# Top-2 gate and dispatch on one core: 15 transfers instead of 24, equal groups of 64 rows, and a share of the multiplication on ScalarE

## The chip, the core and the metric

The kernel runs on one core of one Trainium2 chip. The metric is the device time of one execution in microseconds, as the median of several runs. A profile of one execution (a trace) stands beside it; its span reaches from the first to the last instruction.

## The reference

For each of 16,384 tokens a softmax over 8 router logits is taken, the two largest probabilities are kept and divided by their sum, and the token's row of 512 floats is written twice, each copy multiplied by one of the two weights (the smaller weight first):

```python
# x: [16, 1024, 512] f32, router_logits: [16, 1024, 8] f32, k = 2
probs = softmax(router_logits)
topk_indices = np.argsort(probs, axis=-1)[..., -k:]
topk_probs = np.take_along_axis(probs, topk_indices, axis=-1)
topk_probs = topk_probs / np.sum(topk_probs, axis=-1, keepdims=True)
x_expanded = x[:, :, np.newaxis, :].repeat(k, axis=2)
return (x_expanded * topk_probs[..., np.newaxis]).astype(np.float32)
```

So 33.6 MB of x and 0.5 MB of logits are read and 67.1 MB are written.

## The kernel before

Each of the 128 partitions holds 128 tokens ("rows" below: one row is one token on each partition, 256 KB to load and 512 KB to store over all partitions). The rows come in two groups, GROUPS = [65, 63]; in a group, each partition's rows lie side by side in device memory, so that one transfer has one contiguous piece per partition.

**Buffers.** `xs` holds the x rows of one group, and is used again for the second one. `osp` holds L = 16 output rows. Output rows that have no place in `osp` are written over x rows of `xs` that are no longer needed: `over(r, n, G)` gives the place: two x rows for each output row, from x row 2r - G on.

**Loads.** The x rows of the first group come in six transfers of 2, 4, 2, 8, 17 and 32 rows, those of the second in three of 16, 16 and 31 (LOADS, line 112). After the first two (6 rows) come the logits of all 128 rows, in two transfers (lines 116 and 117). All are issued on SyncE's queue (SP), which works through its instructions in the program's order.

**Weights.** `top2_weights` reduces the 8 logits to the largest and second largest in a tournament of VectorE (DVE) max and min instructions (lines 27 to 40). The two normalised weights are sigmoids of plus and minus their difference, by ScalarE (ACT, lines 42 and 43). This happens once, for all 128 rows.

**Multiplications and stores.** In each group DVE multiplies in pieces, one instruction each (line 128), and each piece is stored by one transfer (line 136): 2 and 14 rows into `osp`, 16 rows over `xs`, two times 8 rows into `osp` again, and the rest over `xs` (9 and 8 rows in the first group, 15 in the second, LAST). The 2-row piece is the early store: it goes out on ACT's queue, all others on SP's. The second use of `osp` waits until its first contents have been stored, and the loads of the second group wait until the output over those rows of `xs` has been stored. Nothing else orders the engines; the framework puts in these waits from the regions that instructions read and write.

Of the kernel before, what the change touches and what calls it, by code (L numbers as in the profile page):

```python
# [1 line left out]

# [4 lines left out]

F32 = mybir.dt.float32
ALU = mybir.AluOpType
ACTF = mybir.ActivationFunctionType  # L10
P = 128


def top2_weights(nc, pool, logits, M, E, tag=""):

    hi, lo, n = None, None, E  # L20
    while n > 1:
        n //= 2
        if hi is None:
            a, b = logits[:, :, 0:n], logits[:, :, n : 2 * n]
            nhi = pool.tile([P, M, n], F32, tag=f"hi{n}{tag}")
            nlo = b
            nc.vector.tensor_tensor(nhi, a, b, op=ALU.max)  # L27
            nc.vector.tensor_tensor(nlo, a, b, op=ALU.min)  # L28
        else:
            a, b = hi[:, :, 0:n], hi[:, :, n : 2 * n]  # L30
            nhi = pool.tile([P, M, n], F32, tag=f"hi{n}{tag}")
            nlo = pool.tile([P, M, n], F32, tag=f"lo{n}{tag}")
            tmp = pool.tile([P, M, n], F32, tag=f"tmp{n}{tag}")
            nc.vector.tensor_tensor(tmp, lo[:, :, 0:n], lo[:, :, n : 2 * n], op=ALU.max)  # L34
            nc.vector.tensor_tensor(nlo, a, b, op=ALU.min)  # L35
            nc.vector.tensor_tensor(nlo, nlo, tmp, op=ALU.max)  # L36
            nc.vector.tensor_tensor(nhi, a, b, op=ALU.max)  # L37
        hi, lo = nhi, nlo
    dlt = pool.tile([P, M], F32, tag=f"dlt{tag}")
    nc.vector.tensor_tensor(dlt, hi[:, :, 0], lo[:, :, 0], op=ALU.subtract)  # L40
    WA = pool.tile([P, M, 2], F32, tag=f"WA{tag}")
    nc.scalar.activation(WA[:, :, 0], dlt, ACTF.Sigmoid, scale=-1.0)  # L42
    nc.scalar.activation(WA[:, :, 1], dlt, ACTF.Sigmoid, scale=1.0)  # L43
    return WA

GROUPS = [65, 63]

LOADS = [[2, 4, 2, 8, 17, 32], [16, 16, 31]]


LAST = [[(48, 9), (57, 8)], [(48, 15)]]


@with_exitstack
def kernel(
    ctx: ExitStack,
    tc: tile.TileContext,  # L60
    x: bass.AP,
    router_logits: bass.AP,
    k: bass.AP,
    out: bass.AP,
):
    nc = tc.nc
    B, S, D = x.shape
    E = router_logits.shape[-1]
    N = B * S
    assert int(k) == 2 and E == 8 and N == P * sum(GROUPS)  # L70
    M = N // P

    L = 16
    x_v, o_v, rl_v = [], [], []
    t0 = 0
    for n in GROUPS:
        t1 = t0 + P * n
        x_v.append(
            x.rearrange("b s d -> (b s) d")[t0:t1].rearrange("(p m) d -> p m d", p=P)
        )  # L80
        o_v.append(
            out.rearrange("b s k d -> (b s) k d")[t0:t1].rearrange(
                "(p m) k d -> p m k d", p=P
            )
        )
        rl_v.append(
            router_logits.rearrange("b s e -> (b s) e")[t0:t1].rearrange(
                "(p m) e -> p m e", p=P
            )
        )  # L90
        t0 = t1

    wpool = ctx.enter_context(tc.tile_pool(name="wpool", bufs=1))
    logits = wpool.tile([P, M, E], F32)
    xs = wpool.tile([P, max(GROUPS), D], F32)
    osp = wpool.tile([P, L, 2, D], F32)

    def over(r, n, G):

        a = 2 * r - G
        return xs[:, a : a + 2 * n, :].rearrange("p (r k) d -> p r k d", k=2)

    h = L // 2
    e = 2
    m0 = 0
    for g, G in enumerate(GROUPS):
        r = 0  # L110
        for n in LOADS[g]:
            nc.sync.dma_start(xs[:, r : r + n, :], x_v[g][:, r : r + n, :])  # L112
            r += n
            if g == 0 and r == 6:

                nc.sync.dma_start(logits[:, :G], rl_v[0])  # L116
                nc.sync.dma_start(logits[:, G:], rl_v[1])
                WA = top2_weights(nc, wpool, logits, M, E)
        assert r == G
        begin = [(0, e, osp[:, :e]), (e, L - e, osp[:, e:])]  # L120
        plan = begin + [
            (L, L, over(L, L, 2 * L)),
            (2 * L, h, osp[:, :h]),
            (2 * L + h, h, osp[:, h:]),
        ]
        plan += [(r, n, over(r, n, G)) for r, n in LAST[g]]
        for r, n, og in plan:
            nc.vector.tensor_tensor(  # L128
                og,
                xs[:, r : r + n, :].unsqueeze(2).to_broadcast([P, n, 2, D]),  # L130
                WA[:, m0 + r : m0 + r + n, :].unsqueeze(3).to_broadcast([P, n, 2, D]),
                op=ALU.mult,
            )

            queue = nc.scalar if n == e else nc.sync
            queue.dma_start(o_v[g][:, r : r + n], og)
        m0 += G


# [1 line left out]
_INS = ['x', 'router_logits', 'k']  # L141
_OUTS = [((16, 1024, 2, 512), 'float32')]

_NUMBERS = {'k': 2}


# [26 lines left out]
```

## Time and profile before

| what | value |
|---|---|
| time, 3 runs | median 240.15 us (239.95 to 240.82) |
| span of the profiled execution | 239.1 us |
| time that lies around the span, by the median | 1.0 us |
| DVE busy | 142.1 us, 24 instructions |
| ACT busy | 1.8 us, 3 instructions |
| moved by DMA | 101.19 MB, mean 423 GB/s over the span |
| SP's queue | 96.5% of the span's DMA time, 3168 packets |
| ACT's queue | 2.1%, 288 packets |

The profiled execution's time is not listed apart from the three runs; its span with 1.0 us around it is taken for the median. The DMA time of a queue is the time that its packets took, as a share of what the 16 DMA engines of the core have in the span. A packet here is one contiguous piece of one partition, or the small write that tells a transfer's end. For a transfer "to landing" is the time from its issue until all 16 engines have reported its end.

### The profile page before, as it was taken

How to read it: one execution, taken by the hardware profiler on the slowest of the kernel's cores; microseconds unless marked ns; L12 is line 12 of the kernel's file. 1: busy time of each engine (PE TensorE's matmuls, PEld its weight loads, DVE VectorE, ACT ScalarE, POOL GpSimd, SP SyncE). 2: the span in 40 equal slices, each digit the busy share in tenths (PEclk: the TensorE clock that was granted, in tenths of full speed). 3: DMA queues.
4: the chain of work that ended last, by engine and by line, in shares of the span. 5: the costliest groups of instructions: out<-in, count | busy, mean ns of one | idle time of the engine just before them, and what ended most of it. 6: DMA issues, size and time to landing. Idle time of an engine off the chain costs nothing.

```text
span 239.1 us, 118 instructions
## 1 busy us (share of the span) xinstructions
DVE 142.1 (59%) x24; ACT 1.8 (1%) x3; POOL 0.2 (0%) x4
## 2 busy tenths in 40 slices
DVE  0589999900299699900000699999006999990000
ACT  2000000000000000000000000000000000000000
POOL 0000000000000000000000000000000000000000
DMA  7999989899999999999999999899899898999894
GB/s 254 440 463 426 441 388 526 329 460 460 417 438 406 400 422 438 438 481 396 433 438 438 438 511 396 384 502 394 384 460 515 362 493 367 428 433 486 380 483 175
DMA packets 3456, 101.19 MB, mean 423 GB/s; under 512 B 384, under 2 KB 512, under 8 KB 896
## 3 DMA queue, kind: packets, MB, share of 16 engines
q1 hardware_dynamic: 3168, 99.09, 96.5%
q10 hardware_dynamic: 288, 2.10, 2.1%
HBM read 34.08 MB, written 67.11 MB: 423 GB/s over the span
## 4 chain that ended last, share of the span: by engine, by line
DMA 52%; DVE 33%; issue 4%; SPq 1%; ACT 0%; DVEq 0%
DMA out_dram<-xs 24%; DVE xs L128 18%; DVE osp L128 13%; DMA out_dram<-osp 13%; DMA xs<-in_x_dram 13%; DMA logits<-in_router_logits_dram 3%; SPq L112 0%; DVE nhi L27 0%; DVE logits L28 0%; DVE nlo L36 0%; DVE nhi L37 0%; DVE nlo L35 0%; DVE tmp L34 0%; SPq L116 0%; ACT WA L42 0%
## 5 line engine op out<-in xcount | busy, mean ns | idle before, releaser
L128 DVE TENSOR_TENSOR osp<-xs,WA 128x8192 f32<-128x8192 f32 (+2 forms) x8 | 69.2, 8688 | 62.3 <-DMA xs<-in_x_dram 31.2
L128 DVE TENSOR_TENSOR xs<-xs,WA 128x16384 f32<-128x16384 f32 (+3 forms) x5 | 69.1, 13811 | 2.2 <-DMA out_dram<-xs 2.0
L27 DVE TENSOR_TENSOR nhi<-logits 128x512 f32<-128x512 f32 x1 | 0.7, 691 | 8.5 <-DMA logits<-in_router_logits_dram 8.5
L42 ACT ACT_TABLE_LOAD x1 | 1.3, 1283 | 0.7 <-PEq L154 0.7
L28 DVE TENSOR_TENSOR logits<-logits 128x512 f32<-128x512 f32 x1 | 0.7, 691 | 0.0
L35 DVE TENSOR_TENSOR nlo<-nhi 128x256 f32<-128x256 f32 (+1 forms) x2 | 0.7, 351 | 0.0
L37 DVE TENSOR_TENSOR nhi<-nhi 128x256 f32<-128x256 f32 (+1 forms) x2 | 0.7, 351 | 0.0
L36 DVE TENSOR_TENSOR nlo<-nlo,tmp 128x256 f32<-128x256 f32 (+1 forms) x2 | 0.7, 350 | 0.0
L34 DVE TENSOR_TENSOR tmp<-logits 128x256 f32<-128x256 f32 x1 | 0.4, 417 | 0.0
L42 ACT ACTIVATE WA<-dlt 128x128 f32<-128x128 f32 x1 | 0.3, 315 | 10.4 <-DVE dlt L40 10.4
L40 DVE TENSOR_TENSOR dlt<-nhi,nlo 128x128 f32<-128x128 f32 x1 | 0.3, 291 | 0.0
L43 ACT ACTIVATE WA<-dlt 128x128 f32<-128x128 f32 x1 | 0.3, 298 | 0.0
L34 DVE TENSOR_TENSOR tmp<-nlo 128x128 f32<-128x128 f32 x1 | 0.3, 283 | 0.0
L154 POOL MEMSET const-bfloat16-1.0<- 128x1 bf16 x1 | 0.1, 101 | 0.0
L154 POOL MEMSET const-uint8-127<- 128x1 uint8 x1 | 0.1, 101 | 0.0
L154 POOL MEMSET const-float32-0.0<- 128x1 f32 x1 | 0.1, 98 | 0.2 <-issue 0.2
L154 POOL MEMSET const-float32-1.0<- 128x1 f32 x1 | 0.1, 98 | 0.0
## 6 DMA issues: line engine op xcount, KB each, us to landing
out_dram<-osp SPq DMA_DIRECT2D x4, 4096.0 KB, 20.7
out_dram<-osp SPq DMA_DIRECT2D x2, 7168.0 KB, 32.4
xs<-in_x_dram SPq DMA_DIRECT2D x2, 4096.0 KB, 30.4
xs<-in_x_dram SPq DMA_DIRECT2D x1, 7936.0 KB, 40.9
out_dram<-xs SPq DMA_DIRECT2D x1, 7680.0 KB, 23.1
out_dram<-xs SPq DMA_DIRECT2D x1, 4608.0 KB, 20.4
xs<-in_x_dram SPq DMA_DIRECT2D x1, 4352.0 KB, 22.8
out_dram<-xs SPq DMA_DIRECT2D x1, 4096.0 KB, 21.4
```

What stands on the lines that cost most here:

```text
L27: nc.vector.tensor_tensor(nhi, a, b, op=ALU.max)
L28: nc.vector.tensor_tensor(nlo, a, b, op=ALU.min)
L34: nc.vector.tensor_tensor(tmp, lo[:, :, 0:n], lo[:, :, n : 2 * n], op=ALU.max)
L35: nc.vector.tensor_tensor(nlo, a, b, op=ALU.min)
L36: nc.vector.tensor_tensor(nlo, nlo, tmp, op=ALU.max)
L37: nc.vector.tensor_tensor(nhi, a, b, op=ALU.max)
L40: nc.vector.tensor_tensor(dlt, hi[:, :, 0], lo[:, :, 0], op=ALU.subtract)
L42: nc.scalar.activation(WA[:, :, 0], dlt, ACTF.Sigmoid, scale=-1.0)
L43: nc.scalar.activation(WA[:, :, 1], dlt, ACTF.Sigmoid, scale=1.0)
L128: nc.vector.tensor_tensor(og, xs[:, r : r + n, :].unsqueeze(2).to_broadcast([P, n, 2, D]), WA[:, m0 + r : m0 + r + n, :].unsqueeze(3).to_b ...
L154: nc = _bacc.Bacc("TRN2", target_bir_lowering=False, num_devices=1)
```

## The change

- GROUPS becomes [64, 64].
- The loads of both groups become 16, 16 and 32 rows. The logits come after the first 16 rows, in one transfer.
- The stores of each group become four of 16 rows: into `osp`, over `xs`, into `osp`, over `xs`. There is no 2-row store on ACT's queue any more; all transfers are on SP's.
- In the third store of each group DVE multiplies 12 rows and ACT the other 4, with eight instructions (each row has two copies) of 512 elements per partition, whose scale is the row's weight.
- The logits and the scratch of the tournament are no tiles of their own: they lie in rows 15 to 17 of `osp`, which has 18 rows now. The weights keep a tile.

The transfers: 3 + 1 + 4 in the first group and 3 + 4 in the second, 15 together, where the kernel before has 8 + 7 and 3 + 6.

```diff
-GROUPS = [65, 63]
-LOADS = [[2, 4, 2, 8, 17, 32], [16, 16, 31]]
-LAST = [[(48, 9), (57, 8)], [(48, 15)]]
+GROUPS = [64, 64]
+M = sum(GROUPS)
+LOADS = [[16, 16, 32], [16, 16, 32]]
+STORES = [
+    [(16, 0, 0), (16, None, 0), (16, 0, 4), (16, None, 0)],
+    [(16, 0, 0), (16, None, 0), (16, 0, 4), (16, None, 0)],
+]
+EARLY = 2
+OSP = 18
...
+    logits = osp[:, OSP - 1].rearrange("p k d -> p (k d)").rearrange("p (m e) -> p m e", e=E)
+    scratch = osp[:, OSP - 3 : OSP - 1].rearrange("p r k d -> p (r k d)")
+    def load_logits():
+        nc.sync.dma_start(
+            logits.rearrange("p (g m) e -> p g (m e)", g=2),
+            rf.rearrange("(g p m) e -> p g (m e)", g=2, p=P),
+        )
...
         for n in LOADS[g]:
             nc.sync.dma_start(xs[:, r : r + n, :], x_v[g][:, r : r + n, :])
+            if g == 0 and r == 0:
+                load_logits()
+                top2_weights(nc, scratch, logits, WA)
             r += n
-            if g == 0 and r == 6:
-                nc.sync.dma_start(logits[:, :G], rl_v[0])
-                nc.sync.dma_start(logits[:, G:], rl_v[1])
-                WA = top2_weights(nc, wpool, logits, M, E)
...
+        for n, home, by_act in STORES[g]:
+            if home is None:
+                a = 2 * r - (r + n)
+                og = xs[:, a : a + 2 * n, :].rearrange("p (r k) d -> p r k d", k=2)
+            else:
+                og = osp[:, home : home + n]
+            v = n - by_act
+            w = WA[:, m0 + r : m0 + r + n, :]
             nc.vector.tensor_tensor(
-                og,
+                og[:, :v],
...
                 op=ALU.mult,
             )
+            for i in range(v, n):
+                for c in range(2):
+                    nc.scalar.activation(
+                        og[:, i, c], xs[:, r + i, :], ACTF.Copy, scale=w[:, i, c : c + 1]
+                    )
+            queue = nc.scalar if n == EARLY else nc.sync
             queue.dma_start(o_v[g][:, r : r + n], og)
+            r += n
```

The tournament in `top2_weights` keeps its instructions and their shapes; only the places of its intermediate results change.

More of the change, by code (lines that the diff above doesn't have):

```diff
@@ L11, with top2_weights, cut @@
 P = 128
-def top2_weights(nc, pool, logits, M, E, tag=""):
-    hi, lo, n = None, None, E
+E = 8
+D = 512
+GROUPS = [64, 64]
[7 more added lines that the diff above has]
+OSP = 18
+def top2_weights(nc, scratch, logits, WA):
+    used = [0]
+    def cut(n):
+        a = scratch[:, used[0] : used[0] + M * n].rearrange("p (m n) -> p m n", n=n)
+        used[0] += M * n
+        return a
+    a, b = logits[:, :, 0:4], logits[:, :, 4:8]
+    hi = cut(4)
+    lo = b
+    nc.vector.tensor_tensor(hi, a, b, op=ALU.max)
+    nc.vector.tensor_tensor(lo, a, b, op=ALU.min)
+    n = 4
@@ L21, in top2_weights @@
     while n > 1:
         n //= 2
[L23 to L37, printed above, removed]
@@ L38, in top2_weights @@
-        hi, lo = nhi, nlo
[L39 to L44, printed above, removed]
-GROUPS = [65, 63]
-LOADS = [[2, 4, 2, 8, 17, 32], [16, 16, 31]]
-LAST = [[(48, 9), (57, 8)], [(48, 15)]]
+        a, b = hi[:, :, 0:n], hi[:, :, n : 2 * n]
@@ new lines, in top2_weights @@
+        nhi, nlo, tmp = cut(n), cut(n), cut(n)
+        nc.vector.tensor_tensor(tmp, lo[:, :, 0:n], lo[:, :, n : 2 * n], op=ALU.max)
+        nc.vector.tensor_tensor(nlo, a, b, op=ALU.min)
+        nc.vector.tensor_tensor(nlo, nlo, tmp, op=ALU.max)
+        nc.vector.tensor_tensor(nhi, a, b, op=ALU.max)
+        hi, lo = nhi, nlo
+    dlt = cut(1)
+    nc.vector.tensor_tensor(dlt, hi, lo, op=ALU.subtract)
+    nc.scalar.activation(WA[:, :, 0], dlt[:, :, 0], ACTF.Sigmoid, scale=-1.0)
+    nc.scalar.activation(WA[:, :, 1], dlt[:, :, 0], ACTF.Sigmoid, scale=1.0)
@@ L66 @@
     nc = tc.nc
[L67 to L73, printed above, removed]
+    N = x.shape[0] * x.shape[1]
+    assert int(k) == 2 and router_logits.shape[-1] == E and x.shape[2] == D
+    assert N == P * M
+    xf = x.rearrange("b s d -> (b s) d")
+    of = out.rearrange("b s k d -> (b s) k d")
+    rf = router_logits.rearrange("b s e -> (b s) e")
     x_v, o_v, rl_v = [], [], []
@@ L77 @@
         t1 = t0 + P * n
-        x_v.append(
-            x.rearrange("b s d -> (b s) d")[t0:t1].rearrange("(p m) d -> p m d", p=P)
-        )
[L81 to L107, printed above, removed]
+        x_v.append(xf[t0:t1].rearrange("(p m) d -> p m d", p=P))
+        o_v.append(of[t0:t1].rearrange("(p m) k d -> p m k d", p=P))
+        rl_v.append(rf[t0:t1].rearrange("(p m) e -> p m e", p=P))
+        t0 = t1
+    pool = ctx.enter_context(tc.tile_pool(name="pool", bufs=1))
+    xs = pool.tile([P, max(GROUPS), D], F32)
+    osp = pool.tile([P, OSP, 2, D], F32)
+    WA = pool.tile([P, M, 2], F32)
+    logits = osp[:, OSP - 1].rearrange("p k d -> p (k d)").rearrange("p (m e) -> p m e", e=E)
[4 more added lines that the diff above has]
+            rf.rearrange("(g p m) e -> p g (m e)", g=2, p=P),
+        )
     m0 = 0
@@ L112 @@
             nc.sync.dma_start(xs[:, r : r + n, :], x_v[g][:, r : r + n, :])
+            if g == 0 and r == 0:
+                load_logits()
+                top2_weights(nc, scratch, logits, WA)
             r += n
-            if g == 0 and r == 6:
-                nc.sync.dma_start(logits[:, :G], rl_v[0])
-                nc.sync.dma_start(logits[:, G:], rl_v[1])
-                WA = top2_weights(nc, wpool, logits, M, E)
         assert r == G
[L120 to L127, printed above, removed]
+        r = 0
+        for n, home, by_act in STORES[g]:
[6 more added lines that the diff above has]
+            w = WA[:, m0 + r : m0 + r + n, :]
             nc.vector.tensor_tensor(
-                og,
-                xs[:, r : r + n, :].unsqueeze(2).to_broadcast([P, n, 2, D]),
-                WA[:, m0 + r : m0 + r + n, :].unsqueeze(3).to_broadcast([P, n, 2, D]),
+                og[:, :v],
+                xs[:, r : r + v, :].unsqueeze(2).to_broadcast([P, v, 2, D]),
+                w[:, :v].unsqueeze(3).to_broadcast([P, v, 2, D]),
                 op=ALU.mult,
             )
-            queue = nc.scalar if n == e else nc.sync
+            for i in range(v, n):
[4 more added lines that the diff above has]
+            queue = nc.scalar if n == EARLY else nc.sync
             queue.dma_start(o_v[g][:, r : r + n], og)
+            r += n
+        assert r == G
         m0 += G
```

## The prediction

> **What bounds the kernel now.** First the page: span, busy times, and what the DMA engines move.
>
> ```profile
> span 239.1 us, 118 instructions
> ...
> DVE 142.1 (59%) x24; ACT 1.8 (1%) x3; POOL 0.2 (0%) x4
> ...
> DMA packets 3456, 101.19 MB, mean 423 GB/s; under 512 B 384, under 2 KB 512, under 8 KB 896
> ```
>
> The busiest engine works 59% of the span. 3456 packets are 24 transfers of 144: 128 pieces, one per partition, and 16 end marks. The mean of 423 GB/s says little by itself; the windows say where it is missed.
>
> ```profile
> core 0: us, DVE busy (x) ACT busy (x) POOL busy (x), PEclk, DMA share, GB/s
> 0.00:8.00 8.00, 0.00 (x0) 1.28 (x1) 0.20 (x4) 1.00 0.78 290
> 20.00:235.00 215.00, 131.23 (x12) 0.00 (x0) 0.00 (x0) 1.00 1.01 435
> 131.20:162.50 31.30, 29.06 (x3) 0.00 (x0) 0.00 (x0) 1.00 1.00 429
> ```
>
> From 20 to 235 us the engines are busy all the time and move 435 GB/s. At that rate the 101.19 MB take 232.6 us, so of the span of 239.1 only 6.5 us are anything else: the start, the end, and small losses in between. The kernel is bound by its bytes, and the change moves the same bytes. It can win a part of 6.5 us, or lose by letting the queue run dry or by a lower rate. So the question is how far ahead of need each transfer is issued. For that I read the timeline, and from the chain of waits and the list of DMA issues one landing each.
>
> ```profile
> 8.53 0.69 DVE L27 TENSOR_TENSOR nhi<-logits 128x512 f32<-128x512 f32 x1 [8.53 <-DMA logits<-in_router_logits_dram]
> ...
> 13.00 17.29 DVE L128 TENSOR_TENSOR osp<-xs,WA 128x2048 f32<-128x2048 f32 x2 [0.58 <-ACT WA L43]
> ...
> 64.42 17.29 DVE L128 TENSOR_TENSOR osp<-xs,WA 128x8192 f32<-128x8192 f32 x2 [16.87 <-DMA out_dram<-osp]
> ...
> 83.74 18.48 DVE L128 TENSOR_TENSOR xs<-xs,WA 128x9216 f32<-128x9216 f32 x2 [2.02 <-DMA out_dram<-xs]
> ...
> 133.41 17.29 DVE L128 TENSOR_TENSOR osp<-xs,WA 128x2048 f32<-128x2048 f32 x2 [31.18 <-DMA xs<-in_x_dram]
> ...
> 181.68 17.29 DVE L128 TENSOR_TENSOR osp<-xs,WA 128x8192 f32<-128x8192 f32 x2 [13.72 <-DMA out_dram<-osp]
> ...
> 215.19 0.33 SPq L136 DMA_DIRECT2D out_dram<-xs  x1
> ```
>
> ```profile
> 93.52 20.37 DMA out_dram<-xs
> ```
>
> ```profile
> out_dram<-xs SPq DMA_DIRECT2D x1, 7680.0 KB, 23.1
> ```
>
> Where DVE waits for a transfer, its start gives that transfer's landing. The bytes up to there (a row is 0.262 MB in, 0.524 MB out) at 435 GB/s give the time that a never-idle queue needs; the difference is how far the queue is behind.
>
> - Logits, start 8.53: 6 rows and the logits, 2.10 MB, 4.8 us: behind 3.7.
> - 14-row store, 64.42: 65 rows, logits, 16 rows out, 25.95 MB, 59.7 us: behind 4.8.
> - 16-row store, 83.74: 34.34 MB, 78.9 us: behind 4.8.
> - 9-row store, 93.52 + 20.37 = 113.89: 25 output rows more, 47.45 MB, 109.1 us: behind 4.8.
> - First load of the second group, 133.41: 55.84 MB, 128.4 us: behind 5.0.
> - 14-row store of the second group, 181.68: 76.55 MB, 176.0 us: behind 5.7.
> - Last store, 215.19 + 23.1 = 238.3: 101.19 MB, 232.6 us: behind 5.7.
>
> This table is the whole budget. 3.7 us are start and landing, and 0.8 us lie between the last landing and the span's end. About 2.0 us are lost on the way, all in the two stretches in which loads end, the early store lies among them, and stores begin (1.1 us up to 64.42, 0.9 us up to 181.68). While stores follow each other, nothing is lost (from 64.42 to 113.89, and from 181.68 to the end), whether of 8 or of 16 rows.
>
> The last store also shows what lead is enough. It is issued at 215.19; the store ahead of it lands one 15-row store earlier, 7.86 MB or 18.1 us before 238.3, at 220.2. The lead of 5.0 us cost nothing.
>
> **The change part by part.** Durations of the multiplications:
>
> ```profile
> L128 DVE TENSOR_TENSOR osp<-xs,WA 128x8192 f32<-128x8192 f32 x4 | 34.6, 8688 | 30.6 <-DMA out_dram<-osp 30.6
> L128 DVE TENSOR_TENSOR xs<-xs,WA 128x16384 f32<-128x16384 f32 x2 | 34.4, 17224 | 0.1
> ...
> L42 ACT ACT_TABLE_LOAD x1 | 1.3, 1283 | 0.7 <-PEq L154 0.7
> ...
> L42 ACT ACTIVATE WA<-dlt 128x128 f32<-128x128 f32 x1 | 0.3, 315 | 10.4 <-DVE dlt L40 10.4
> ```
>
> 8 rows take 8.69 us and 16 take 17.22, so one takes 1.07, and 12 take 12.96. I go through the new queue with the table's losses left in (behind 4.8 in the first group, 5.7 in the second), the harder case for every lead.
>
> *Loads, logits, weights.* The logits lie behind 16 rows: 4.72 MB, 10.8 us, behind 3.7, landing at 14.6 (before: 8.5). The tournament and the sigmoids keep their 13.00 - 8.53 = 4.5 us; the weights come at 19.1. The first multiplication of 16 rows ends at 36.3, and its store is issued then. The cover is the loads themselves: 64 rows and logits are 17.30 MB, 39.8 us, landing at 44.6. Lead 8.3. That the first store waits for 16 rows instead of 2 thus costs nothing; without that cover it would cost the 15 us of the other 14 rows.
>
> *Second store.* DVE goes on from 36.3 to 53.5. The first store lands at 25.69 MB, 59.1 + 4.8 = 63.9. Lead 10.4.
>
> *Third store, and ACT's part.* It needs `osp` free at 63.9. DVE takes 12.96 us for 12 rows. ACT's eight instructions of 512 elements are not in the trace; the nearest row has 128 elements in 0.315 us. From below, nothing but a fixed part: 8 x 0.3 = 2.4 us; from above, all of it by the element: 8 x 1.26 = 10.1 us, and 11.4 with another table load. Either way it ends before DVE, whose 12.96 us hide it, and ACT has nothing else queued. I take 5 us; it doesn't enter. The store is issued at 76.9; the second one lands 19.3 us after the first, at 83.2. Lead 6.3, more than the 5.0 that was enough. With all 16 rows on DVE it would be 2.1, less than any lead seen.
>
> *Fourth store.* It waits for no transfer, DVE follows at once: 94.1. The third lands at 102.5. Lead 8.4. The loads of the second group are issued right behind it on SP; two of them wait for the second store (83.2, past), the third for the fourth store's landing at 121.8. At that point two loads, 19.3 us of work, are still queued. SP's order holds nothing up: no store of the second group is ready before.
>
> *Second group.* The first load lands 9.6 us after the fourth store, at 131.7 with the table's 0.2; the multiplication ends at 148.9, the loads at about 161. Lead 12. From there the first group's distances repeat: leads of about 14, 6.3 and 8.4. So DMA's queue never runs dry, and DVE's freed time (the removed instructions, four rows of each third store) buys nothing.
>
> *What the fewer transfers bring.* Two bounds. From below, zero: where stores queue plainly, three transfers (25 rows, 83.74 to 113.89, 30.15 us) take what the 16-row store's 19.32 us (64.42 to 83.74) give for 25 rows, 30.2. From above, the 2.0 us lost, if the early stores and small loads cause all of it. Neither is likely whole: both passages from loads to stores remain, the early stores in them go. Spread evenly over the 20 transfers behind the logits the loss is 0.10 us each; the change has 13 behind its logits, so 7 x 0.10 = 0.7. I take 0.65. The start (3.7) and end (0.8) I leave as they are.
>
> The sum: span 239.1 - 0.65 = 238.5. The median of the runs is 240.15, 1.0 us above the span, so 239.5 us.
>
> A rule of the Trainium skill speaks for far more: "DMA: Bandwidth & Descriptors", section "Anatomy of one DMA", gives about 2.0 us of fixed cost to each DMA. By that figure nine fewer would save an estimated 18 us if none overlapped; the row of 435 GB/s over 215 us leaves no room for it, and the trace decides.
>
> **The rivals.**
>
> *Faster by over 0.5%.* 0.5% is 1.2 us, about what a measurement of this kernel can tell from no change. If the early stores' mixing with the loads is what costs, 1.2 to 2.0 us go: 238.2 to 238.95. For it: both losses lie where an early store is. Against: both also lie at the passage from loads to stores, which stays.
>
> *Slower, a lower rate.* With 64 rows the partitions' pieces begin at whole multiples of 128 KB in x and 256 KB in the output; before, 130 and 126, 260 and 252 KB. If such even distances send the engines to the same part of memory together, every transfer is slower. No row shows it; the lowest rate over a long stretch is 429 GB/s (131.2 to 162.5), by which 101.19 MB take 235.9 us, 3.2 more: 242.7 us with the gain. It decides as soon as the rate in plain stretches falls below 432. Against: the 435 hold through loads, stores and both at once alike, which speaks for a limit in the DMA engines and not in the memory.
>
> The Trainium skill has this as a rule against the change, in "DMA: Bandwidth & Descriptors", section "Latency and other measured facts": distances at large powers of two slow a copy, from 214 GB/s to 207 at 512 KiB and more at larger ones, and 4 KiB of padding restores it. By an estimate from that page, 3.4% of 232.6 us is 7.9 us; it gives no figure for 128 or 256 KiB, and no run here shows one.
>
> *Slower, ACT behind DVE.* If ACT's rows of the third store don't run beside DVE's but after them (both write one buffer), that store comes after 12.96 + 2.4 to 10.1 us, 6 in the middle: 19.0 after the landing. It decides from 19.3 - 5.0 = 14.3 us on; past that the queue may stand still up to 4.7 us in each group. Half of that is 4.7 together: 244.2 us. Against: DVE writes pieces of `xs` while loads to other pieces of it run, so regions are told apart.
>
> **How the numbers follow.** Forecast, within 0.5%: 0.66, 239.5 us, its own range 238.95 to 240.7. All losses gone: 0.17. Lower rate: 0.11. ACT behind DVE: 0.06. So faster 0.17, same 0.66, slower 0.17. The range from 238.3 to 242.5 takes in the forecast, nearly all of the faster case and about half of the lower rate's, and leaves out some 0.14.
>
> **What would show it.** Right: 2288 packets; 435 GB/s from 20 us to near the end; DVE's first multiplication near 19 and ACT's eight instructions within DVE's 13 us; the stores' landings 19.3 us apart; the queue between 5.0 and 5.5 us behind at the end. Wrong: landings over 19.4 us apart while stores follow each other (the rate); a window near 80 or 196 us clearly under 435 (the third store late); behind under 4.5 at the end (the early stores were the loss).

## The result and the profile after

| | time, median | runs | ratio to before, 95% interval |
|---|---|---|---|
| before | 240.21 us (239.95 to 240.82) | 15 | |
| changed | 240.81 us (240.50 to 241.20) | 15 | 1.0023 [1.0015, 1.0031] |

Here and below, executions more than 1.5% above the fastest of their kernel are left out of the ratios.

The change costs 0.6 us, 0.23%. That is within 0.5%, but clear of noise, and it is a loss where a gain of 0.65 us was forecast. First the changed kernel's page and timeline, in the order of the prediction's steps; then one window of 215 us; the last line is the time from issue to landing of its last store, from the list of DMA issues.

```profile
span 239.0 us, 116 instructions
...
DVE 133.1 (56%) x19; ACT 11.8 (5%) x19; POOL 0.2 (0%) x4
...
DMA packets 2288, 101.19 MB, mean 423 GB/s; under 512 B 240, under 2 KB 240, under 8 KB 496
```

```profile
18.71 17.22 DVE L119 TENSOR_TENSOR osp<-xs,WA 128x16384 f32<-128x16384 f32 x1 [0.58 <-ACT WA L58]
...
63.78 12.96 DVE L119 TENSOR_TENSOR osp<-xs,WA 128x12288 f32<-128x12288 f32 x1 [10.59 <-DMA out_dram<-osp]
63.80 5.01 ACT L127 ACTIVATE osp<-xs,WA 128x512 f32<-128x512 f32 x8 [45.12 <-DMA out_dram<-osp]
76.81 0.33 SPq L131 DMA_DIRECT2D out_dram<-osp  x1
...
131.66 17.23 DVE L119 TENSOR_TENSOR osp<-xs,WA 128x16384 f32<-128x16384 f32 x1 [37.59 <-DMA xs<-in_x_dram]
...
180.33 12.96 DVE L119 TENSOR_TENSOR osp<-xs,WA 128x12288 f32<-128x12288 f32 x1 [14.18 <-DMA out_dram<-osp]
...
210.63 0.33 SPq L131 DMA_DIRECT2D out_dram<-xs  x1
```

```profile
20.00:235.00 215.00, 127.98 (x8) 10.03 (x16) 0.00 (x0) 1.00 1.00 431
```

```profile
out_dram<-xs SPq DMA_DIRECT2D x1, 27.5
```

All that lies off the queue came as worked out: 2288 packets, the first multiplication at 18.7 (19.1 forecast), ACT's eight instructions in 5.01 us beside DVE's 12.96, the third store issued at 76.8 (76.9). The window's 431 GB/s, where 435 was forecast, says little: a slower kernel below (before_64, 241.22 us) shows 435 in the same window, so the pieces that happen to end inside it count for that much, and the landings are the better measure.

The span is 239.0, and not 0.6 us longer than the 239.1 of before, while the runs differ by 0.6. The profiled run took 240.82 us, 1.8 around its span. All later runs that list both numbers also have 1.7 to 1.8 us around the span. So the profile of before, with 239.1, is not of an execution of 240.2 us but of one near 240.9. A second profile of the kernel before was of a run of 240.16 us (page, timeline and last landing):

```profile
span 238.4 us, 118 instructions
```

```profile
63.99 17.29 DVE L128 TENSOR_TENSOR osp<-xs,WA 128x8192 f32<-128x8192 f32 x2 [16.44 <-DMA out_dram<-osp]
...
133.02 17.29 DVE L128 TENSOR_TENSOR osp<-xs,WA 128x2048 f32<-128x2048 f32 x2 [31.23 <-DMA xs<-in_x_dram]
...
180.92 17.29 DVE L128 TENSOR_TENSOR osp<-xs,WA 128x8192 f32<-128x8192 f32 x2 [13.35 <-DMA out_dram<-osp]
...
214.43 0.33 SPq L136 DMA_DIRECT2D out_dram<-xs  x1
```

```profile
out_dram<-xs SPq DMA_DIRECT2D x1, 7680.0 KB, 23.1
```

The prediction's measure is how far the queue is behind: the time of a landing, less the time that the bytes up to there take at 435 GB/s. These rows give it at four points. A: the first 16 output rows have landed (DVE starts on the third store). C: the second group's first load has landed. D: that group's first 16 output rows have landed. E: the last landing. The bytes take 59.1, 126.6, 174.8 and 232.6 us with 64-row groups, 59.7, 128.4, 176.0 and 232.6 with 65 and 63.

| us behind at | A | C | D | E | growth from A to D |
|---|---|---|---|---|---|
| before, first profile (a longer run) | 4.8 | 5.0 | 5.7 | 5.7 | 0.9 |
| before, second profile | 4.3 | 4.7 | 4.9 | 4.9 | 0.6 |
| changed | 4.7 | 5.1 | 5.6 | 5.5 | 0.9 |

Against the common execution of before the changed kernel is 0.6 us further behind at the end, and that is its loss: 0.4 are there at A, another 0.2 by D. Between A and C the queue passes from stores to loads, before A and before D from loads to stores; I call these the passages. From D to E, stores only, nothing is lost in either kernel. Each line of the table is one execution, and the two of before differ by as much as 0.8 us, so differences of 0.2 or 0.3 us between single profiles prove little. The question for the experiments was what makes the passages dearer.

### The profile page after: what moved, and what is told of

Same layout as the page of the kernel before. It is cut to its first block, busy times and chain, and to the rows that moved or that the text cites. A ratio compares the mean times of both kernels' runs of the same rounds, so it can differ in the third digit from the quotient of the medians.

```text
span 239.0 us, 116 instructions
## 1 busy us (share of the span) xinstructions
DVE 133.1 (56%) x19; ACT 11.8 (5%) x19; POOL 0.2 (0%) x4
## 2 busy tenths in 40 slices
DMA packets 2288, 101.19 MB, mean 423 GB/s; under 512 B 240, under 2 KB 240, under 8 KB 496
## 3 DMA queue, kind: packets, MB, share of 16 engines
q1 hardware_dynamic: 2288, 101.19, 98.7%
## 4 chain that ended last, share of the span: by engine, by line
DMA 46%; DVE 41%; SPq 0%; issue 0%; ACT 0%; DVEq 0%
DVE osp L119 25%; DMA out_dram<-osp 25%; DMA xs<-in_x_dram 16%; DVE xs L119 14%; DMA osp<-in_router_logits_dram 5%; DVE osp L43 0%; DVE osp L44 0%; DVE osp L52 0%; DVE osp L51 0%; DVE osp L53 0%; DVE osp L50 0%; SPq L104 0%; SPq L131 0%; ACT WA L57 0%; DVE osp L56 0%
## 5 line engine op out<-in xcount | busy, mean ns | idle before, releaser
L119 DVE TENSOR_TENSOR osp<-xs,WA 128x16384 f32<-128x16384 f32 (+1 forms) x4 | 60.4, 15092 | 62.9 <-DMA xs<-in_x_dram 37.6
L119 DVE TENSOR_TENSOR xs<-xs,WA 128x16384 f32<-128x16384 f32 x4 | 68.9, 17225 | 0.3
L127 ACT ACTIVATE osp<-xs,WA 128x512 f32<-128x512 f32 x16 | 10.0, 708 | 156.7 <-DMA out_dram<-osp 156.7
L43 DVE TENSOR_TENSOR osp<-osp 128x512 f32<-128x512 f32 x1 | 0.7, 691 | 14.2 <-DMA osp<-in_router_logits_dram 14.2
L57 ACT ACTIVATE WA<-osp 128x128 f32<-128x128 f32 x1 | 0.3, 316 | 16.2 <-DVE osp L56 16.2
L44 DVE TENSOR_TENSOR osp<-osp 128x512 f32<-128x512 f32 x1 | 0.7, 691 | 0.0
L51 DVE TENSOR_TENSOR osp<-osp 128x256 f32<-128x256 f32 (+1 forms) x2 | 0.7, 352 | 0.0
L53 DVE TENSOR_TENSOR osp<-osp 128x256 f32<-128x256 f32 (+1 forms) x2 | 0.7, 352 | 0.0
L50 DVE TENSOR_TENSOR osp<-osp 128x256 f32<-128x256 f32 (+1 forms) x2 | 0.7, 352 | 0.0
L52 DVE TENSOR_TENSOR osp<-osp 128x256 f32<-128x256 f32 (+1 forms) x2 | 0.7, 351 | 0.0
L58 ACT ACTIVATE WA<-osp 128x128 f32<-128x128 f32 x1 | 0.3, 298 | 0.0
```

What stands on the lines that cost most here:

```text
L43: nc.vector.tensor_tensor(hi, a, b, op=ALU.max)
L44: nc.vector.tensor_tensor(lo, a, b, op=ALU.min)
L57: nc.scalar.activation(WA[:, :, 0], dlt[:, :, 0], ACTF.Sigmoid, scale=-1.0)
L58: nc.scalar.activation(WA[:, :, 1], dlt[:, :, 0], ACTF.Sigmoid, scale=1.0)
L119: nc.vector.tensor_tensor(og[:, :v], xs[:, r : r + v, :].unsqueeze(2).to_broadcast([P, v, 2, D]), w[:, :v].unsqueeze(3).to_broadcast([P, v ...
L127: nc.scalar.activation(og[:, i, c], xs[:, r + i, :], ACTF.Copy, scale=w[:, i, c : c + 1])
```

## Experiments

Each was run beside the kernel before on the same chip, and ratios are to before. Four chips were used. The kernel before took 240.20 to 240.29 us on each, but the changed one took 240.81 us in one place and 241.14 in another. So a ratio is the safer number, and a difference of 0.2 or 0.3 us between two medians from different chips shows nothing by itself.

Four theories were tested. P: the even distances of 64-row groups cost (the partitions' pieces begin 128 KB apart in x and 256 KB apart in the output). E: the missing early store costs. H: the long last piece of a load costs. L: the late issue of the first store costs. The names of the runs are explained below the table.

| run | median us | ratio, 95% interval |
|---|---|---|
| again_before | 240.17 | 1.0005 [0.9993, 1.0016] |
| again_after (the changed kernel) | 241.14 | 1.0031 [1.0020, 1.0041] |
| rows65_63 | 240.37 | 1.0000 [0.9986, 1.0014] |
| before_64 | 241.22 | 1.0034 [1.0021, 1.0047] |
| distance_double | 243.12 | 1.0118 [1.0104, 1.0132] |
| early_back | 240.56 | 1.0011 [1.0003, 1.0020] |
| before_no_early | 240.52 | 1.0011 [1.0002, 1.0019] |
| rows65_63_early | 240.55 | 1.0014 [1.0005, 1.0022] |
| loads16 | 240.59 | 1.0015 [1.0007, 1.0024] |
| logits_first | 241.12 | 1.0034 [1.0022, 1.0047] |
| rows65_63_logits_first | 242.39 | 1.0082 [1.0065, 1.0099] |
| before_merged | 240.22 | 1.0001 [0.9992, 1.0010] |
| no_act | 243.77 | 1.0138 [1.0117, 1.0159] |
| rows65_63_no_act | 242.00 | 1.0068 [1.0056, 1.0080] |
| rows65_63_halves | 240.82 | 1.0021 [1.0012, 1.0030] |
| before_merged_no_act | 241.51 | 1.0053 [1.0033, 1.0073] |
| two_queues | 244.29 | 1.0174 [1.0137, 1.0211] |
| before_merged_two_queues | 241.29 | 1.0024 [0.9994, 1.0054] |

**The two kernels again.**

> The kernel before, unchanged, profiled once more, to see how well its one profile stands for its runs. If the profile of before is of a common execution: 240.2 us and a span of 239.1. If it is of one of the longer executions: 240.2 us at a span near 238.4, that is 1.8 us around the span as in the changed kernel, and the two hand-overs from loads to stores cheaper than in the first profile. Then the change lost 0.6 us in the span as well.

> The changed kernel unchanged, beside the runs that follow it on the same chip. If its loss is the same everywhere: 240.7 to 240.9 us, the passages stretched as in its first profile. If what the even distances cost differs from chip to chip or from load to load: another time, between 240.5 and 242 us, and the difference lies at the passages.

For before it was the second case: a span of 238.4 at 240.16 us, 1.8 around it. The changed kernel on another chip took 241.14 us; its profile is behind by 4.6, 5.0, 5.9 and 6.0, so the growth from A to D is 1.3 us instead of 0.9. The size of the loss is not the same everywhere, nor how it is shared between the passages; its sign is, and from D to E again nearly nothing is lost.

**Even distances: undone, put into the kernel before, doubled.**

```diff
# rows65_63 (changed kernel; logits in two transfers)
-GROUPS = [64, 64]
+GROUPS = [65, 63]
-LOADS = [[16, 16, 32], [16, 16, 32]]
+LOADS = [[16, 17, 32], [16, 16, 31]]
...   last stores: 9 and 8 rows; 15 rows
# before_64 (kernel before)
-GROUPS = [65, 63]
+GROUPS = [64, 64]
-LOADS = [[2, 4, 2, 8, 17, 32], [16, 16, 31]]
+LOADS = [[2, 4, 2, 8, 16, 32], [16, 16, 32]]
-LAST = [[(48, 9), (57, 8)], [(48, 15)]]
+LAST = [[(48, 8), (56, 8)], [(48, 16)]]
# distance_double (changed kernel)
-        x_v.append(xf[t0:t1].rearrange("(p m) d -> p m d", p=P))
+        x_v.append(xf.rearrange("(p m) d -> p m d", p=P)[:, t0:t1])
...   the same for out; logits as 128 pieces of 4 KB
```

> The changed kernel with groups of 65 and 63 rows: loads 16, 17, 32 and 16, 16, 31, stores of 16, 16, 16, 9, 8 and of 16, 16, 16, 15; the logits in two transfers, since the groups differ. Theory P: 0.6 us or more gained, 240.0 to 240.3 us, and 16-row stores landing closer than 19.3 us. Theories H and E: two more transfers, 240.8 to 241.0; the stretches at the passages as in the changed kernel.

> The kernel before with groups of 64 and 64 rows and nothing else (loads 2, 4, 2, 8, 16, 32 and 16, 16, 32; last stores 8, 8 and 16): 24 transfers as before, early store kept. Theory P (the even distances make each passage between loads and stores dearer): 240.6 to 240.8 us. Theory E alone (the missing early store): 240.2 us, as the kernel before.

> The changed kernel with another deal of the tokens: each partition has 128 tokens side by side, and the groups are the first and the second 64 of them. All transfers keep their sizes; the partitions' pieces begin 256 KB apart in x and 512 KB in the output, twice as far and as even as in the changed kernel (the logits are 128 pieces of 4 KB now). Theory P: slower still, 241.3 us or more, the loss at the passages or in the rate of the plain stores. Theories L and E: 240.8 us as the changed kernel. By a figure of the Trainium skill, page DMA: Bandwidth & Descriptors, section Latency and other measured facts (512 KiB: 207 instead of 214 GB/s), it would be an estimated 7 us.

The rows of the timelines, first rows65_63, then before_64, then distance_double:

```profile
64.17 12.96 DVE L115 TENSOR_TENSOR osp<-xs,WA 128x12288 f32<-128x12288 f32 x1 [10.81 <-DMA out_dram<-osp]
...
133.07 17.23 DVE L115 TENSOR_TENSOR osp<-xs,WA 128x16384 f32<-128x16384 f32 x1 [31.09 <-DMA xs<-in_x_dram]
...
180.95 12.96 DVE L115 TENSOR_TENSOR osp<-xs,WA 128x12288 f32<-128x12288 f32 x1 [13.40 <-DMA out_dram<-osp]
```

```profile
63.72 17.29 DVE L128 TENSOR_TENSOR osp<-xs,WA 128x8192 f32<-128x8192 f32 x2 [16.12 <-DMA out_dram<-osp]
...
131.69 17.29 DVE L128 TENSOR_TENSOR osp<-xs,WA 128x2048 f32<-128x2048 f32 x2 [33.22 <-DMA xs<-in_x_dram]
...
180.77 17.29 DVE L128 TENSOR_TENSOR osp<-xs,WA 128x8192 f32<-128x8192 f32 x2 [14.53 <-DMA out_dram<-osp]
```

```profile
64.09 12.96 DVE L115 TENSOR_TENSOR osp<-xs,WA 128x12288 f32<-128x12288 f32 x1 [10.93 <-DMA out_dram<-osp]
...
133.26 17.23 DVE L115 TENSOR_TENSOR osp<-xs,WA 128x16384 f32<-128x16384 f32 x1 [38.89 <-DMA xs<-in_x_dram]
...
182.59 12.96 DVE L115 TENSOR_TENSOR osp<-xs,WA 128x12288 f32<-128x12288 f32 x1 [14.84 <-DMA out_dram<-osp]
```

Behind at A, C, D: 4.5, 4.7, 5.0 with 65 and 63 rows; 4.7, 5.1, 6.0 for before with 64; 5.0, 6.7, 7.8 with doubled distances. The growth from A to D is 0.5, 1.4 and 2.8 us. All three go the way of P and against the others: undoing it takes 0.44 us off the changed kernel, putting it into the kernel before adds 1.0 us, doubling it adds 2.3. And it is not the rate of plain stores. In distance_double the second, third and fourth stores are issued and land as these rows of its timeline and of its list of issues say. The second and the third land 19.3 us apart (53.19 + 30.1 = 83.3, 77.12 + 25.5 = 102.6), as 16 rows do in the kernel before. The fourth, which has loads behind it, lands 21.2 us after the third (94.40 + 29.4 = 123.8); in the changed kernel that is 19.9 us:

```profile
53.19 0.34 SPq L127 DMA_DIRECT2D out_dram<-xs  x1
...
77.12 0.33 SPq L127 DMA_DIRECT2D out_dram<-osp  x1
94.40 0.33 SPq L127 DMA_DIRECT2D out_dram<-xs  x1
```

```profile
out_dram<-xs SPq DMA_DIRECT2D x1, 30.1
...
out_dram<-osp SPq DMA_DIRECT2D x1, 25.5
...
out_dram<-xs SPq DMA_DIRECT2D x1, 29.4
```

The rule that the Trainium skill gives in "DMA: Bandwidth & Descriptors", section "Latency and other measured facts", thus holds in its direction; the 7.9 us estimated from it do not, and the measurement decides. Even in distance_double, whose output distance is the page's 512 KiB, the loss against the kernel before is 2.8 us, and it is paid around the passages. Why it is paid there the runs don't show, nor whether the distances in x or those in the output cause it.

**The early store.**

```diff
# early_back (changed kernel), rows65_63_early (rows65_63)
-(16, 0, 0)
+(2, 0, 0), (14, 2, 0)
# before_no_early (kernel before)
-begin = [(0, e, osp[:, :e]), (e, L - e, osp[:, e:])]
+begin = [(0, L, osp[:, :L])]
```

> The changed kernel with the early store of 2 rows on ACT's queue put back in both groups (stores of 2, 14, 16, 16 and 16 rows). Theory E: the passages cost as little as in the kernel before, 240.2 to 240.4 us. Theories H and P: two more transfers, 240.8 to 241.0.

> The kernel before with its first two stores of each group as one of 16 rows on SP's queue: no early store, 22 transfers, first store issued near 30 us as before. Theory E: the passages become dearer by 0.5 to 1 us together, 240.5 to 241.0 us. Theories L and P: two transfers less, 0.1 to 0.2 us gained, 240.0 us.

> The changed kernel with both undone that cost by P and E: groups of 65 and 63 rows, and the early store of 2 rows on ACT's queue. It keeps large loads, 16-row stores and ACT's part; 19 transfers. If P and E add up (0.4 and 0.25 us off the changed kernel's 240.8, five transfers less than before): 240.0 to 240.2 us, the passages as in the kernel before. If one of them takes the place of the other: 240.4 us as with 65 and 63 rows alone.

With 64 rows the early store takes 0.25 us off the changed kernel, and without it the kernel before loses 0.3. But in the changed kernel with 65 and 63 rows it adds 0.2 instead. Only the second of these differences is clear of noise (1.0002 to 1.0019); in the other two pairs the intervals overlap. So it is not shown to be a cause with a sign of its own, and P and E don't add up. One thing speaks against a fixed price for P: with the early store, 64 rows (early_back, 240.56) and 65 and 63 rows (rows65_63_early, 240.55) take the same time, on two chips. So what the even distances cost depends on something that these runs leave open.

**The last load's piece and the first store's issue.**

```diff
# loads16 (changed kernel)
-LOADS = [[16, 16, 32], [16, 16, 32]]
+LOADS = [[16, 16, 16, 16], [16, 16, 16, 16]]
# logits_first (changed kernel; also with 65 and 63 rows)
+            if g == 0 and r == 0:
+                load_logits()
             nc.sync.dma_start(xs[:, r : r + n, :], x_v[g][:, r : r + n, :])
             if g == 0 and r == 0:
-                load_logits()
                 top2_weights(nc, scratch, logits, WA)
```

> The changed kernel with the loads of each group as 16, 16, 16 and 16 rows, so that the last load in front of the stores has pieces of 32 KB instead of 64. Theory H (each passage from loads to stores stretches the last piece of every DMA engine, the more the longer that piece is): the stretch falls by about half in both groups, 0.5 to 0.7 us less, two more transfers cost 0.1: 240.2 to 240.4 us. Theory E (the missing early store is what costs) and theory P (the even distances of 64-row groups cost): nothing gained, 240.8 to 240.95.

> The changed kernel with the logits' transfer ahead of the first load of 16 rows, nothing else. The weights are there some 9 us earlier, DVE begins when the first 16 rows land near 14 us, and the first store is issued near 31 us instead of 36, some 9 us ahead of the passage instead of 4. Theory L (the first passage is dear because its store is issued late, 4 us ahead; the kernel before issues it 13 us ahead): the last load piece of the first group is stretched by about 0.5 us instead of 1.0, 240.3 us. Theories P (even distances) and E (no early store): 240.8 us, the stretch unchanged.

> Groups of 65 and 63 rows as in the run before, and the logits ahead of the first load. If P and L each hold for their part: 239.8 to 240.0 us, under the kernel before (240.2). If only P: 240.4 as with 65 and 63 rows alone.

loads16 is 0.2 us faster than the changed kernel, a third of what H expected, on another chip and with overlapping intervals; H is not shown. L falls: issuing the first store 4.6 us earlier gained nothing. The third kernel was a miss for both of its expectations: 2 us slower. In its profile DVE gets the first 16 rows at 16.3 us instead of 14.1 as in logits_first, and stays as late. From A to D it loses 0.5 us, the same as rows65_63, so these 2 us lie in the first loads and say nothing of the passages. Their cause is open.

**Fewer transfers alone.**

```diff
# before_merged (kernel before)
-LOADS = [[2, 4, 2, 8, 17, 32], [16, 16, 31]]
+LOADS = [[2, 4, 10, 17, 32], [16, 16, 31]]
-            (2 * L, h, osp[:, :h]),
-            (2 * L + h, h, osp[:, h:]),
+            (2 * L, L, osp),
...   ACT multiplies the last 4 of these 16 rows
```

> The kernel before with three transfers less and nothing else moved: the loads of 2 and 8 rows as one of 10, and the two 8-row stores as one of 16 in both groups, of which ACT multiplies 4 rows. Early store and groups of 65 and 63 stay. By the packets alone 0.2 us less than before: 240.0 us. If fewer transfers bring nothing whatever: 240.2 us.

Nothing, within about 0.2 us either way; at the prediction's 0.10 us for each transfer three fewer would have gained 0.3. Together with rows65_63, which has 17 transfers and a ratio of 1.0000, this tests the term that I had at 0.65 us.

**ACT's part and the lead of the third store.**

```diff
# no_act (changed kernel), rows65_63_no_act (rows65_63)
-(16, 0, 4)
+(16, 0, 0)
# rows65_63_halves (rows65_63)
-(16, 0, 4)
+(8, 0, 0), (8, 8, 0)
# before_merged_no_act: before_merged with all 16 rows on DVE
```

> The changed kernel with all 16 rows of the third stores on DVE. The third store is then issued 17.2 us after the first one's landing, 2.1 us ahead of the second one's landing. If a lead of 2.1 us is too short, the queue stands still in both groups: 0.5 to 2 us slower, 241.3 to 243 us, a gap between the second and the third store's landings above 19.3. If it is enough: 240.8 us, and ACT's part brings nothing.

> Groups of 65 and 63 rows in the changed kernel, all rows of the third stores on DVE. Without ACT's part the kernel with 64-row groups took 243.8 us. If that is the late issue of the third store (about 2 us ahead of the second one's landing): 3 us over the 240.4 of 65 and 63 rows with ACT, 243.0 to 243.5 us. If it is the even distances that grew dearer there: 240.3 to 240.6 us, as with ACT.

> Groups of 65 and 63 rows in the changed kernel, ACT's part away, and each third store in two halves of 8 rows, so that the first half is issued 8.7 us after the landing instead of 17.2. If it is the short lead of the third store that makes the later passages dear (rows65_63_no_act: 242.0 us, 0.8 us at each of the later two passages): they are cheap again, 240.4 to 240.6 us. If ACT's absence itself does it: 242 us.

> The kernel before with three transfers less, as in an earlier run (240.2 us), but all 16 rows of the third stores on DVE: a lead of about 2 us there. If the short lead makes the later passages dear, it does so with the early store and uneven groups too: 241.5 to 242 us, with 0.7 to 0.9 us at the passages near 120 and 158 us. If not: 240.2 us.

Without ACT's part the changed kernel takes 243.8 us, 2.6 more than with it on the same chip (241.14). That isn't paid where I looked for it. Rows of no_act, timeline and list of issues:

```profile
53.15 0.34 SPq L131 DMA_DIRECT2D out_dram<-xs  x1
63.77 17.23 DVE L119 TENSOR_TENSOR osp<-xs,WA 128x16384 f32<-128x16384 f32 x1 [10.64 <-DMA out_dram<-osp]
81.02 0.33 SPq L131 DMA_DIRECT2D out_dram<-osp  x1
...
132.52 17.23 DVE L119 TENSOR_TENSOR osp<-xs,WA 128x16384 f32<-128x16384 f32 x1 [34.26 <-DMA xs<-in_x_dram]
...
182.03 17.23 DVE L119 TENSOR_TENSOR osp<-xs,WA 128x16384 f32<-128x16384 f32 x1 [15.02 <-DMA out_dram<-osp]
```

```profile
out_dram<-xs SPq DMA_DIRECT2D x1, 29.8
...
out_dram<-osp SPq DMA_DIRECT2D x1, 21.3
```

The second store lands at 53.15 + 29.8 = 83.0, the third is issued 2.0 us before that and lands at 102.3, 19.3 us after the second: no gap. But the queue is behind by 6.0 at C and 7.3 at D, where the changed kernel has 5.1 and 5.6. (The profiled run, 242.53 us, was the shortest of the five; the others took 243.8 to 244.0, and what they lost beyond it no profile shows.) The same shows with uneven groups, in rows65_63_no_act and in before_merged_no_act:

```profile
64.45 17.23 DVE L115 TENSOR_TENSOR osp<-xs,WA 128x16384 f32<-128x16384 f32 x1 [10.96 <-DMA out_dram<-osp]
...
133.90 17.22 DVE L115 TENSOR_TENSOR osp<-xs,WA 128x16384 f32<-128x16384 f32 x1 [31.63 <-DMA xs<-in_x_dram]
...
182.50 17.23 DVE L115 TENSOR_TENSOR osp<-xs,WA 128x16384 f32<-128x16384 f32 x1 [14.12 <-DMA out_dram<-osp]
```

```profile
64.47 17.23 DVE L129 TENSOR_TENSOR osp<-xs,WA 128x16384 f32<-128x16384 f32 x1 [16.84 <-DMA out_dram<-osp]
...
134.14 17.30 DVE L129 TENSOR_TENSOR osp<-xs,WA 128x2048 f32<-128x2048 f32 x2 [31.80 <-DMA xs<-in_x_dram]
...
182.41 17.23 DVE L129 TENSOR_TENSOR osp<-xs,WA 128x16384 f32<-128x16384 f32 x1 [13.71 <-DMA out_dram<-osp]
```

Behind at A, C and D: 4.8, 5.5, 6.5 and 4.8, 5.8, 6.4, a growth of 1.7 and 1.6 us where the same kernels with ACT's part, rows65_63 and before_merged, grow by 0.5 and 0.6. rows65_63_halves has no ACT either, but issues the first half 8.7 us after the landing:

```profile
64.38 17.29 DVE L115 TENSOR_TENSOR osp<-xs,WA 128x8192 f32<-128x8192 f32 x2 [11.14 <-DMA out_dram<-osp]
73.10 8.93 SPq L127 DMA_DIRECT2D out_dram<-osp  x2
...
133.39 17.22 DVE L115 TENSOR_TENSOR osp<-xs,WA 128x16384 f32<-128x16384 f32 x1 [31.22 <-DMA xs<-in_x_dram]
...
181.23 17.30 DVE L115 TENSOR_TENSOR osp<-xs,WA 128x8192 f32<-128x8192 f32 x2 [13.35 <-DMA out_dram<-osp]
```

It is behind by 4.7, 5.0 and 5.2, a growth of 0.5, and takes 240.82 us: 1.2 less than rows65_63_no_act, though 0.2 above what was expected if the lead alone mattered. So most of it is the short lead, not ACT's absence, and it makes the later passages dearer, 20 us and more after the store that came late. By what means the profiles don't show; it stays open. ACT's part is worth its place in the changed kernel: it keeps the lead at 6 us. The two kernels without ACT's part are also a pair for P on one chip: 243.77 us with 64 rows, 242.00 with 65 and 63.

**Loads and stores on two queues.**

```diff
# two_queues (changed kernel), before_merged_two_queues (before_merged, there n == e)
-            queue = nc.scalar if n == EARLY else nc.sync
+            queue = nc.scalar
```

> The changed kernel with all stores on ACT's queue and the loads alone on SP's: nothing else. Loads and stores then run side by side around both passages, and no engine turns from one to the other at a sharp point. If a passage is dear because all engines turn together: the stretches go, 239.6 to 240.2 us. If reading and writing at the same time is what the even distances make dear: every piece in the mixed stretches is slower, 241.5 us or more.

> The kernel before with three transfers less (240.2 us in an earlier run), and all stores on ACT's queue. With groups of 65 and 63 rows mixing costs little by theory P: the first passage (about 0.5 us) goes, 239.6 to 240.0 us. If mixing itself is dear: above 240.5 us.

Mixing is no cure. With even distances it costs 3.1 us against the changed kernel on the same chip (244.3 against 241.1; single runs from 242.4 to 245.8). With uneven ones the 12 runs scatter from 240.2 to 244.6 us (the table's median is of all 12), and the comparison is undecided. No version beats the kernel before. before_merged equals it; so does rows65_63 within its interval, with a median 0.17 us above.

## Why the prediction was wrong

*What bounds the kernel: right.* The leads of the second, third and fourth store were 10.6, 6.2 and 8.2 us, worked out as 10.4, 6.3 and 8.4. No store came late, and the loss lies in the few microseconds beside the 232.6 of the bytes.

*The budget: mis-sized by its baseline.* I took a profile with a span of 239.1 for one of the median, 240.15, and so put 1.0 us around it. It was 1.8 us, and the profile one of a longer execution. The queue's 2.0 us lost on the way, from which the gain was cut, were about 1.2 in the common execution (4.9 at the end, 3.7 at the logits). So the sign that I had set for a right forecast, 5.0 to 5.5 us behind at the end, was met (5.5) by luck of that baseline, and meant a loss.

*The step that failed: "what the fewer transfers bring".* I spread the loss evenly over the transfers, 0.10 us each, and took 0.65 for seven of them. My own lower bound, from plain stores, said zero, and zero is what was measured: before_merged 240.22 us, rows65_63 a ratio of 1.0000. The loss belonged to the passages, where the table had shown it, and not to the number of transfers. That both passages from loads to stores stay was in the text; the third, from stores to loads, was only carried along with the table's 0.2 us. And the sum had no term for the even distances at all; their 0.44 us are most of the measured loss of 0.6.

The 2.0 us for each DMA, rightly set aside, did not fit the case in the first place: in the Trainium skill, "DMA: Bandwidth & Descriptors", the section "Anatomy of one DMA" fits them to transfers that GpSimd issues, and all transfers here are on SP's and ACT's queues.

*The rival that came true, at another price and place.* Even distances cost 0.44 us in the changed kernel and 1.0 in the kernel before. I had them lower the rate of every transfer, 3.2 us, and gave that a chance of 0.11. The rate of plain stores stayed (19.3 us per 16 rows); the passages paid. The sign I had set out for it, landings over 19.4 us apart among stores, would have missed it; only the fourth store, with loads behind it, came later than that (19.9). The sum that the runs would give: 240.2, fewer transfers 0, even distances +0.44, and 0.2 left, which lies within the interval of rows65_63: 240.8.

*ACT behind DVE: did not happen.* Its eight instructions ran beside DVE. But the rival's point, that a short lead is dear, holds more than I thought: about 2 us of lead in place of 6 cost 1.3, 1.6 and 2.6 us in three kernels (by the ratios).

## What to carry to other kernels

In this kernel the DMA queue is always full, and nothing was lost between stores; what was left to win or lose lay where loads and stores change over. So in such a kernel try pieces off even distances, and keep each store's issue several microseconds ahead (6 us was enough here, 2 was not). Before a gain of a microsecond is cut from one profile, hold that profile's span against the spans of other runs. Merging transfers of 0.5 MB and more gained nothing here by itself.

## What the runs showed of the hardware

- A passage between loads and stores loses time though the queue is full, 0.2 to 1.7 us in these profiles. A 16-row store with stores around it lands 19.2 to 19.4 us after the one ahead of it in the kernels with all loads and large stores on one queue; one with loads behind it took 19.9 us in the changed kernel, and 21.2 with doubled distances.
- Even distances of 128 KB in x and 256 KB in the output cost 0.44 and 1.0 us in two kernels, 1.8 in a pair without ACT's part, and nothing measurable in a pair with the early store. Twice these distances cost 2.3 us more. Stores between stores kept their rate.
- A store issued 2.0 us before the one ahead of it lands causes no gap there, but dearer passages later, 1.3 to 2.6 us together. Why is open.
- ACT's multiplication of 512 elements by a weight per partition takes 0.71 us by itself (708 ns in the row below, from the groups by line and form of the changed kernel). Eight in a row take 5.01 us, less than eight times that, so they overlap.

```profile
L127 ACT ACTIVATE osp<-xs,WA 128x512 f32<-128x512 f32 x16 | 10.0, 708 | 156.7 <-DMA out_dram<-osp 156.7
```
